# Queries and keys split once on 128 partitions and placed into the heads' stacked operands by transfers

## The chip, the cores and the metric

The kernel runs on one core of a Trainium2 chip. The metric is device time in microseconds (us) for one launch. Engines are named as in the profile: PE is TensorE (PEld its weight loads), DVE is VectorE, ACT is ScalarE, POOL is GpSimd, SP is SyncE, which here issues almost all transfers.

## The reference

One sequence of 512 tokens of width 1024 and 256 context tokens pass through two blocks of two layers each, all in float32. The first block's layers project to three kinds of heads, attend, project back and run an MLP with squared relu:

```python
q_a = _apply_rope(_heads(a_q, A_HEADS), cos64, sin64)
k_a = _apply_rope(_heads(a_k, A_KV_HEADS), cos64, sin64)
y_a = _window_attn(q_a, k_a, v_a, k_a_ctx, v_a_ctx, sink_a)
q_b = _apply_rope(_rms_norm(_heads(b_q, B_HEADS), q_norm_b), cos64, sin64)
k_b = _apply_rope(_rms_norm(_heads(b_k, B_KV_HEADS), k_norm_b), cos64, sin64)
...
def mla_q(cq):
    q = _heads(_rms_norm(cq, mla_q_norm) @ w_uq, C_HEADS)
    return q[..., :C_NOPE_DIM], q[..., C_NOPE_DIM:]
...
y = jnp.concatenate([_merge(y_a), _merge(y_b), _merge(y_c)], axis=-1) @ w_out
```

A heads (4 of 64, with 2 key heads) attend in a window with a sink, B heads (4, with 2 key heads) and C heads (8, with 64 rows without and 32 with rotation) to all 768 tokens. The second block's first layer adds a differential attention and a hyena (a gated long convolution), its second a pool over windows; both have MLPs:

```python
def _diff_attn(q, k, v, lam):
    s = jnp.einsum("bqhcd,bkhcd->bhcqk", q, k, preferred_element_type=jnp.float32) * (ATT_QK_DIM ** -0.5)
    p = jax.nn.softmax(s, axis=-1)
    w = p[:, :, 0] - lam * p[:, :, 1]
    return jnp.einsum("bhqk,bkhd->bqhd", w.astype(v.dtype), v)
```

## The kernel before

Activations stand with features on partitions and tokens in the row (512, or 768 with the context). Every operand of a product is kept as two float32r parts, hi and lo: `split` writes hi with ACT and lo = x − hi with DVE. `mm3` (L649) makes the products hi·hi, hi·lo and lo·hi of each 128-row piece; L656 is their matmul. Weights come through `Stream` in pieces of 128x1024: a load on SP (L79), hi on ACT (L97), lo on DVE (L98).

For queries and keys of 64 rows the two parts of a head are stacked on the 128 partitions, so that one product takes both. `k_post` (L753) writes for each of two key heads the rows [hi; lo] (L762, L763) and [lo; hi] (L764, L765), `q_post` (L740) for each of two query heads [hi; lo] (L749, L750). All of these are operations on 64 partitions, and those that cross halves read one half and write the other. `stack_key` (L1488, L1489) and `stack_query` (L1497 to L1500) do the same for the differential attention's keys and queries, `c_pair` (L877) prepares two C heads, rows [64; 32], from PSUM by `split` (L662, L663 for keys, L665, L666 for queries). The rotated 32 rows are made in u and w and go into the operands by transfers (`dma`, L669, on SP), as the keys' rotated rows kr do.

Tiles come from pools: `Tm` gives one of 4 slots of 128x768 (raw and temporary values: w, u, kx, qx, lam, the first component's probabilities), `B` one of 21 slots of 128x1536. A slot is taken again once the last reader of what it held is done.

Work is written unit by unit. `attend` (L916) runs units of 128 queries of one head as a pipeline: scores (L264), maximum (DVE L277), exponential (ACT L287), normalising (POOL L296), transposes (L310), their split (ACT L337, DVE L342), products with the values (L353). B heads come first, then A, then C; the pairs of C heads are prepared by `prepare` in steps between the units of the heads before:

```python
start = nab * 5 // 8 if p == 0 else nab + (p - 1) * per + 4
if i == start:
    gens[p] = prepare(p)
```

Beside the projections and the attention run background jobs: `mod_job` (weights wm loaded by SP, L597; multiplied on POOL, L580; summed on ACT, L581, or on DVE, L584), `context_job` (the differential attention's context keys) and the filter's job. In `mixer` (L1666) the keys, values and queries of the differential attention are projected between the steps of the hyena's chain (L1840: ka, x0, hy); then lam is loaded (L1772), and attention 2 begins. A scheduler sets each engine's order of instructions once, when the program is built; at run time each engine, SP included, works through its list in order.

Of the kernel before, what the change touches and what calls it, by code (L numbers as in the profile page):

```python
# [11 lines left out]
F32 = mybir.dt.float32  # L12
F32R = mybir.dt.float32r
# [51 lines left out]
class Stream:  # L65
    """Weight pieces [128, 1024] in the order of their use: loaded ahead, split into two float32r parts."""
# [45 lines left out]
class SideStream:  # L112
    """Weight pieces [128, 512] for work beside the main stream, three to a slot of the big pool."""
# [19 lines left out]
class Packer:  # L133
    """Views of a fixed width, several to a slot of the pool."""
# [17 lines left out]
class LayerNorm:  # L152
    """Norm over the rows of z (8 tiles of 128 rows) for one range of tokens; stats of the sums run with the producer."""
# [44 lines left out]
class RmsNorm:  # L198
    """Norm without mean; the squares are summed as the producer goes, the last ones (or all) by products."""
# [30 lines left out]
class Pair:  # L230
    """Transposed probabilities of two blocks of queries: [key, slot, 256 queries], hi and lo."""
# [9 lines left out]
class Unit:  # L241
    """One block of 128 queries of one head against its keys (or, for the context, both blocks at once)."""
# [74 lines left out]
    def parts(self):  # L317
        """(psum view, destination slots) of this block's transposed probabilities."""
# [45 lines left out]
class DiffUnit(Unit):  # L364
    """One block of 128 queries of one component of a differential head; the second one combines the two."""
# [39 lines left out]
class Kernel:  # L405
# [19 lines left out]
    def psum(self, pairs, singles):  # L425
        """PSUM as so many pairs of banks and so many single ones."""
# [6 lines left out]
    # ---------------------------------------------------------------- tiles  # L433
# [30 lines left out]
    def norm_space(self, n):  # L464
        """Three rows of n; two narrow ones that follow each other share a slot."""
# [8 lines left out]
    # ---------------------------------------------------------------- background  # L474
# [13 lines left out]
    def run(self, gen, rate=0, jobs=0):  # L488
        """gen, with so many steps of modulation and of other jobs (on average) after each of its own."""
# [9 lines left out]
    def weave(gens):  # L499
        """The generators' steps in turn."""  # L500
# [8 lines left out]
    @staticmethod  # L509
    def drain(gen):  # L510
        """Runs a generator to its end and returns its value."""
        while True:
            try:
                next(gen)
            except StopIteration as e:
                return e.value
# [7 lines left out]
    # ---------------------------------------------------------------- start  # L524
# [30 lines left out]
    def bcast(self, v, slot):  # L555
        """sbc[:, slot, :] = silu vector v on every partition."""
# [1672 lines left out]
```

## Time and profile before

| what | value |
|---|---|
| three runs | 3031.02, 3032.82, 3033.07 us; median 3032.82 |
| profiled execution | span 3033.6 us, 0.8 us above the median; its time outside the span is not listed apart |
| granted TensorE clock, mean | 0.964 of full speed |
| busy share of the span | PE 92%, DVE 68%, ACT 42%, POOL 26% |
| data moved | 327.80 MB, mean 108 GB/s |

The profiled execution is one run of its own. Busy shares are means over stages with different limits; what an edit is worth is read from its stage. In the rows below a line with `x4` is a group of four instructions of one kind that followed each other, with its first start and their total time, and the brackets at a line's end give the idle time before it and what ended that.

### The profile page before, as it was taken

To read this page: it belongs to the slowest core of one execution; us is meant where nothing else is said; L and a number is where in the kernel's file an instruction comes from. 1 tells how busy PE (TensorE), PEld (TensorE's weight loads), DVE (VectorE), ACT (ScalarE), POOL (GpSimd) and SP (SyncE) were. 2 spreads that over 40 slices of the span, in tenths; PEclk is the share of its full clock that TensorE was granted. 3 is DMA by queue.
4 is the path that set the end of the run, shared out by engine and by line. 5 is a ranking of instruction groups with operands and counts; after the bars stand their busy time and mean duration, and the time that the engine had idled before them with its cause. 6 is when DMAs were issued, how large, how long until landed. Compare 5 with 4: busy or idle time off the path is not lost.

```text
span 3033.6 us, 39799 instructions
## 1 busy us (share of the span) xinstructions
PE 2802.4 (92%) x14828; PEld 2352.8 (78%) x14828; DVE 2072.6 (68%) x3213; ACT 1262.5 (42%) x2282; POOL 777.9 (26%) x870
## 2 busy tenths in 40 slices
PE   6868989999999989888999999988899999699998
PEld 4757878888888878777887788766688888588887
DVE  5788876776556676887687565677976754764444
ACT  3557883412222235777332333533653223343222
POOL 4354456401000060343601122343211000400001
PEclk8979999999999999999999999999999999799999
DMA  5320122254444411012255565333125533123332
GB/s 233 106 77 12 35 82 70 91 154 145 150 131 129 125 63 60 11 33 73 64 174 178 177 204 174 102 128 108 59 68 193 200 124 98 46 84 97 96 97 71
DMA packets 102492, 327.80 MB, mean 108 GB/s; under 512 B 11643, under 2 KB 18747, under 8 KB 102300
## 3 DMA queue, kind: packets, MB, share of 16 engines
q1 hardware_dynamic: 101724, 323.56, 33.1%
q8 instruction: 117, 1.92, 0.3%
q10 hardware_dynamic: 576, 1.70, 0.2%
q14 instruction: 75, 0.61, 0.1%
HBM read 306.09 MB, written 13.37 MB: 105 GB/s over the span
## 4 chain that ended last, share of the span: by engine, by line
PE 70%; DVE 13%; issue 6%; ACT 5%; POOL 3%; DMA 2%; SPq 0%; DVEq 0%; POOLq 0%; ACTq 0%
PE f L656 47%; PE op L656 6%; PE pj L656 5%; PE s L264 3%; PE acc L353 2%; PE pt L310 1%; ACT p L287 1%; DVE st L277 1%; DVE h L1081 1%; DVE wlo L98 1%; DVE ptl L342 1%; DVE junk L584 1%; ACT pth L337 1%; PE lv L187 1%; DVE R L181 1%
## 5 line engine op out<-in xcount | busy, mean ns | idle before, releaser
L97 ACT CAST whi<-wraw 128x1024 fp32r<-128x1024 f32 x342 | 357.8, 1047 | 1190.7 <-PE f L656 1007.8
L656 PE MATMUL f<-hn,whi 128*128 128x512 f32 (+1 forms) x2688 | 716.9, 364 | 8.3 <-ACT hn L1082 6.3
L98 DVE TENSOR_TENSOR wlo<-wraw,whi 128x1024 fp32r<-128x1024 f32 x342 | 433.8, 1268 | 355.8 <-ACT whi L97 348.6
L656 PE MATMUL f<-act,whi 128*128 128x512 f32 x2240 | 613.0, 371 | 2.6 <-DVE R L983 2.6
L656 PEld LDWEIGHTS f<-hn,whi 128*128 128x128 f32 x2688 | 466.7, 190 | 95.1 <-ACT hn L1082 8.4
L656 PEld LDWEIGHTS f<-act,whi 128*128 128x128 f32 x2240 | 390.5, 189 | 79.7 <-DVE R L983 4.2
L656 PE MATMUL f<-hn,wlo 128*128 128x512 f32 (+1 forms) x1344 | 445.7, 361 | 0.0
L656 PE MATMUL f<-act,wlo 128*128 128x512 f32 x1120 | 377.7, 370 | 0.0
L570 POOL COPY wm<-act 128x1 f32<-128x1 f32 x152 | 81.1, 540 | 826.5 <-ACT act L945 419.3
L983 DVE SCALAR_TENSOR_TENSOR R<-f,modsb,R 128x512 f32<-128x512 f32 (+1 forms) x280 | 188.7, 693 | 130.8 <-PE f L656 130.6
L584 DVE SCALAR_TENSOR_TENSOR wm<-wm,sbc 128x1024 f32<-128x1024 f32 x152 | 186.5, 1228 | 128.2 <-DMA wm<-wada_in 80.7
L656 PEld LDWEIGHTS f<-hn,wlo 128*128 128x128 f32 x1344 | 237.2, 189 | 39.3
L656 PE MATMUL pj<-h,whi 128*128 128x512 f32 x864 | 241.1, 379 | 21.9 <-ACT h L662 17.7
L656 PEld LDWEIGHTS f<-act,wlo 128*128 128x128 f32 x1120 | 194.5, 188 | 36.7
L656 PEld LDWEIGHTS pj<-h,whi 128*128 128x128 f32 x864 | 151.1, 193 | 59.5 <-ACT h L662 19.0
L296 POOL TENSOR_SCALAR p<-p,st 128x768 f32<-128x768 f32 (+2 forms) x160 | 132.4, 831 | 195.1 <-DVE st L294 159.1
L277 DVE TENSOR_REDUCE st<-s 128x1 f32<-128x768 f32 (+3 forms) x176 | 155.9, 889 | 24.8 <-PE s L264 17.4
L342 DVE TENSOR_TENSOR ptl<-pt,pth 128x256 fp32r<-128x256 f32 (+3 forms) x304 | 152.8, 535 | 23.2 <-ACT pth L337 20.7
L218 POOL TENSOR_TENSOR ns<-ns,rq 128x256 f32<-128x256 f32 x54 | 46.9, 878 | 455.4 <-ACT rq L210 454.5
L310 PE MATMUL pt<-ident,p 128*128 128x128 f32 x816 | 127.0, 285 | 21.5 <-POOL p L296 13.1
L656 PE MATMUL pj<-h,wlo 128*128 128x512 f32 (+1 forms) x432 | 141.4, 370 | 0.0
L337 ACT CAST pth<-pt 128x256 fp32r<-128x256 f32 (+3 forms) x304 | 128.7, 471 | 30.1 <-PE pt L310 21.9
(375 smaller groups left out, 4836.1 us busy)
## 6 DMA issues: line engine op xcount, KB each, us to landing
wraw<-fc_in SPq DMA_DIRECT2D x128, 512.0 KB, 3.8
wraw<-mlp_in SPq DMA_DIRECT2D x128, 512.0 KB, 3.6
wm<-wada_in SPq DMA_DIRECT2D x96, 512.0 KB, 3.9
wm<-wmod_in SPq DMA_DIRECT2D x80, 512.0 KB, 3.8
wraw<-win_in SPq DMA_DIRECT2D x24, 512.0 KB, 3.7
wraw<-wout_in SPq DMA_DIRECT2D x16, 512.0 KB, 3.8
wraw<-mixhy_in SPq DMA_DIRECT2D x12, 512.0 KB, 3.7
wn<-wmodn_in SPq DMA_DIRECT2D x8, 512.0 KB, 7.7
```

The costliest lines, as they stand in the source:

```text
L97: nc.scalar.copy(out=hi[:, 0:n], in_=t[:, 0:n])
L98: nc.vector.tensor_tensor(out=lo[:, 0:n], in0=t[:, 0:n], in1=hi[:, 0:n].bitcast(F32), op=ALU.subtract)
L264: nc.tensor.matmul(self.s[:, a:b], lhsT=q, rhs=kk[:, k0:k0 + b - a], start=i == 0, stop=end)
L277: nc.vector.tensor_reduce(out=self.st[:, 0:self.nq], in_=s, axis=AX.X, op=ALU.max, negate=True)
L296: nc.gpsimd.tensor_scalar(out=self.p[:, b * m:b * m + m], in0=self.p[:, b * m:b * m + m], scalar1=st[:, 6 + b:7 + b], scalar2=1.0, op0=ALU ...
L310: nc.tensor.transpose(self.pt[t // w][:, t % w * 128:t % w * 128 + 128], self.p[:, t * 128:t * 128 + 128], k.ident)
L337: self.k.nc.scalar.copy(out=pr.hi[:, s0:s0 + c, q0:q0 + nq], in_=src)
L342: self.k.nc.vector.tensor_tensor(out=pr.lo[:, s0:s0 + c, q0:q0 + nq], in0=src, in1=pr.hi[:, s0:s0 + c, q0:q0 + nq].bitcast(F32), op=ALU.su ...
L570: self.nc.gpsimd.tensor_copy(out=t[:, 0:1], in_=self.gate)
L584: nc.vector.scalar_tensor_tensor(out=junk, in0=t, scalar=1.0, in1=s, op0=ALU.mult, op1=ALU.mult, accum_out=dst)
L656: self.nc.tensor.matmul(ps[:, c0:c1], lhsT=w, rhs=x[:, c0:c1], start=first and n == 0, stop=last and n == 2)
L983: nc.vector.scalar_tensor_tensor(out=zz, in0=ps[:, c0:c1], scalar=g(m0 + mi), in1=zz, op0=ALU.mult, op1=ALU.add)
```

## The change

A helper `halves` splits a tile of two heads once, on all 128 partitions: hi into a slot of `Tm`, lo in place of the tile. The parts are then copied into the stacked operands by transfers on SP, one for each 64 rows. The diff also takes out comments and docstrings; line numbers after it are up to 12 higher.

```diff
+    def halves(self, X, n, scale=None):
+        hi, lo = self.Tm("hs")[:, 0:n].bitcast(F32R), X[:, 0:n].bitcast(F32R)
+        self.split(hi, lo, X[:, 0:n], scale)
+        return hi, lo
...
     def q_post(self, X, q2, N, ranges, gain):
...
+        hi, lo = self.halves(X, N, SC64)
         for hd in range(2):
             a, b = slice(64 * hd, 64 * hd + 64), slice(64 - 64 * hd, 128 - 64 * hd)
-            x, hi = X[a, 0:N], q2[a, hd, 0:N]
-            nc.scalar.activation(out=hi, in_=x, func=AF.Copy, scale=SC64)
-            nc.vector.scalar_tensor_tensor(out=q2[b, hd, 0:N], in0=x, scalar=SC64, in1=hi.bitcast(F32), op0=ALU.mult, op1=ALU.subtract)
+            self.dma(q2[a, hd, 0:N], hi[a])
+            self.dma(q2[b, hd, 0:N], lo[a])
...
     def k_post(self, X, kk, gain):
...
+        hi, lo = self.halves(X, T)
         for hd in range(2):
             a, b = slice(64 * hd, 64 * hd + 64), slice(64 - 64 * hd, 128 - 64 * hd)
-            x, hi = X[a, :], kk[hd][a, 0, :]
-            nc.scalar.copy(out=hi, in_=x)
-            nc.vector.tensor_tensor(out=kk[hd][b, 0, :], in0=x, in1=hi.bitcast(F32), op=ALU.subtract)
-            nc.scalar.copy(out=kk[hd][b, 1, :], in_=x)
-            nc.vector.tensor_tensor(out=kk[hd][a, 1, :], in0=x, in1=hi.bitcast(F32), op=ALU.subtract)
+            self.dma(kk[hd][a, 0, :], hi[a])
+            self.dma(kk[hd][b, 0, :], lo[a])
+            self.dma(kk[hd][b, 1, :], hi[a])
+            self.dma(kk[hd][a, 1, :], lo[a])
...
     def c_pair(self, wq, wkv, cq, ckv, kr, j, qs, ks, ranges):
...
+        parts = [self.Tm("cq")[:, 0:N].bitcast(F32R) for _ in range(2)]
+        self.split(*parts, pn[:, 0:N], SC96)
         for i in range(2):
-            self.split(qs[i][0:64, 0, 0:N], qs[i][0:64, 1, 0:N], pn[64 * i:64 * i + 64, 0:N], SC96)
+            for n in range(2):
+                self.dma(qs[i][0:64, n, 0:N], parts[n][64 * i:64 * i + 64])
...
+        parts = [self.Tm("ck").bitcast(F32R) for _ in range(2)]
+        self.split(*parts, pk[:, 0:T])
         for i in range(2):
-            self.split(ks[i][0:64, 0, :], ks[i][0:64, 1, :], pk[64 * i:64 * i + 64, 0:T])
+            for n in range(2):
+                self.dma(ks[i][0:64, n, :], parts[n][64 * i:64 * i + 64])
             self.dma(ks[i][64:96, :, :], kr[64:96, :, :])
...
     def stack_key(self, x, d):
+        hi, lo = self.halves(x, x.shape[-1])
...
-            nc.scalar.copy(out=d[c][own], in_=x[own])
-            nc.vector.tensor_tensor(out=d[c][oth], in0=x[own], in1=d[c][own].bitcast(F32), op=ALU.subtract)
+            self.dma(d[c][own], hi[own])
+            self.dma(d[c][oth], lo[own])
...
     def stack_query(self, x, d, e):
+        hi, lo = self.halves(x, x.shape[-1], SC64)
...
-            hi = d[c][own].bitcast(F32)
-            nc.scalar.activation(out=d[c][own], in_=x[own], func=AF.Copy, scale=SC64)
-            nc.scalar.activation(out=e[c][oth], in_=x[own], func=AF.Copy, scale=SC64)
-            nc.vector.scalar_tensor_tensor(out=d[c][oth], in0=x[own], scalar=SC64, in1=hi, op0=ALU.mult, op1=ALU.subtract)
-            nc.vector.scalar_tensor_tensor(out=e[c][own], in0=x[own], scalar=SC64, in1=hi, op0=ALU.mult, op1=ALU.subtract)
+            self.dma(d[c][own], hi[own])
+            self.dma(d[c][oth], lo[own])
+            self.dma(e[c][oth], hi[own])
+            self.dma(e[c][own], lo[own])
```

How the change moves instructions is shown at three places. The first is the start of layer 0's attention. On DVE, before (kk are the stacked keys of the B heads, q_1072 and q_1073 the stacked queries of the A heads, raw the projected tiles, s scores):

```order
L763 TENSOR_TENSOR kk<-raw,kk 64x768
L765 TENSOR_TENSOR kk<-raw,kk 64x768
L763 TENSOR_TENSOR kk<-raw,kk 64x768
L765 TENSOR_TENSOR kk<-raw,kk 64x768
L738 TENSOR_TENSOR raw<-raw,w 128x512 x2
L277 TENSOR_REDUCE st<-s 128x1
L750 SCALAR_TENSOR_TENSOR q_1072<-raw,q_1072 64x768 x2
L750 SCALAR_TENSOR_TENSOR q_1073<-raw,q_1073 64x768 x2
```

and on DVE now:

```order
L663 TENSOR_TENSOR raw<-raw,hs 128x768
L737 TENSOR_TENSOR w<-rot,tab 128x512
L738 TENSOR_TENSOR raw<-raw,w 128x512
L737 TENSOR_TENSOR w<-rot,tab 128x512
L738 TENSOR_TENSOR raw<-raw,w 128x512
L666 SCALAR_TENSOR_TENSOR raw<-raw,hs 128x768
L584 SCALAR_TENSOR_TENSOR junk,modsb<-wm,sbc 128x1024
L666 SCALAR_TENSOR_TENSOR raw<-raw,hs 128x768
```

Four operations on kk have become one, four on q two. On SP the place now reads, at its end, where kk are the A heads' (before, eight wm loads stood there one behind the other, with no transfer of kk or q):

```order
L669 DMA kk<-hs 64x768
L669 DMA kk<-raw 64x768
L669 DMA kk<-hs 64x768
L669 DMA kk<-raw 64x768
L597 DMA wm<-wmod_in 128x1024 x3
L669 DMA qc<-cq 64x768 x4
L669 DMA kc<-kr 32x1536
```

Three of the wm loads now stand behind the 24 placing transfers of that place. The second place is SP in layer 1's attention, where a pair of C heads is prepared (qc, kc are the heads' operands, w and u the two parts of the rotated rows). Before:

```order
L669 DMA kc<-kr 32x1536 x2
L669 DMA qc<-w 32x512
L669 DMA qc<-u 32x512
L669 DMA qc<-w 32x512
L669 DMA qc<-u 32x512
L669 DMA kc<-kr 32x1536
```

and now:

```order
L669 DMA qc<-cq 64x512 x4
L669 DMA kc<-kr 32x1536
L669 DMA qc<-w 32x512
L669 DMA qc<-u 32x512
L669 DMA qc<-w 32x512
L669 DMA qc<-u 32x512
L669 DMA kc<-ck 64x768 x4
L669 DMA kc<-kr 32x1536
```

The keys' four pieces stand behind the four of the rotated rows. The third place is SP ahead of attention 2. Before:

```order
L79 DMA wraw<-mixq_in 128x1024 x2
L79 DMA wraw<-mixout_in 128x1024 x4
L1772 DMA lam<-lam_in 128x256
L1820 DMA hyr<-hy 128x512 x4
L1317 DMA R<-xb 128x512 x8
```

and the end of it now (hs and qx are hi and lo of a query tile, q_18707 and q_18708 stacked operands):

```order
L669 DMA q_18707<-hs 64x512
L669 DMA q_18707<-qx 64x512
L669 DMA q_18708<-hs 64x512
L669 DMA q_18708<-qx 64x512
L1783 DMA lam<-lam_in 128x256
L79 DMA wraw<-mixout_in 128x1024 x2
L1831 DMA hyr<-hy 128x512 x4
```

The load of lam has moved behind all 32 transfers of the queries.

## Rows read from the trace of the kernel before

**Rows 1.** page: busy time by engine, and the chain's shares by engine

```profile
PE 2802.4 (92%) x14828; PEld 2352.8 (78%) x14828; DVE 2072.6 (68%) x3213; ACT 1262.5 (42%) x2282; POOL 777.9 (26%) x870
PE 70%; DVE 13%; issue 6%; ACT 5%; POOL 3%; DMA 2%; SPq 0%; DVEq 0%; POOLq 0%; ACTq 0%
```

**Rows 2.** stretches: us, busy by engine (x count), granted clock, DMA share, GB/s

```profile
178.00:200.00 22.00, 9.95 (x20) 4.62 (x20) 19.34 (x20) 11.18 (x16) 12.79 (x7) 0.64 0.21 65
1224.00:1240.00 16.00, 9.21 (x36) 6.88 (x36) 14.47 (x24) 11.15 (x21) 4.50 (x5) 0.68 0.10 33
1280.00:1420.00 140.00, 123.90 (x778) 107.08 (x776) 110.67 (x236) 101.87 (x246) 56.50 (x64) 0.94 0.18 50
2127.00:2145.00 18.00, 10.73 (x46) 7.89 (x46) 17.28 (x33) 9.94 (x20) 4.02 (x4) 0.81 0.11 37
2700.00:2800.00 100.00, 100.00 (x443) 82.81 (x442) 48.07 (x56) 30.23 (x38) 0.00 (x0) 1.00 0.33 98
```

**Rows 3.** lines: durations ns min/median/max, first and last start, forms

```profile
L763 DVE TENSOR_TENSOR kk<-raw,kk x8: 952/954/3025, 186.2 to 1231.8; 64x768 fp32r<-64x768 f32 x8
L663 DVE TENSOR_TENSOR ckv<-raw,ckv x2: 954/956/959, 117.2 to 1174.0; 128x768 fp32r<-128x768 f32 x2
L666 DVE SCALAR_TENSOR_TENSOR qc<-cn,qc x16: 673/816/960, 273.3 to 1392.3; 64x768 fp32r<-64x768 f32 x8, 64x512 fp32r<-64x512 f32 x8
```

**Rows 4.** DMA issues: queue, count, KB each, median us to landing

```profile
kc<-kr SPq DMA_DIRECT2D x16, 192.0 KB, 2.7
qc<-w SPq DMA_DIRECT2D x8, 96.0 KB, 2.1
lam<-lam_in SPq DMA_DIRECT2D x1, 128.0 KB, 3.4
```

**Rows 5.** tile qc, SP's issues from 260 to 420: durations ns

```profile
L669 SPq DMA_DIRECT2D qc<-w x8: 507/519/582, 283.4 to 402.6; - x8
```

**Rows 6.** timeline of VectorE and POOL: start, us, engine, line, operation

```profile
186.22 3.02 DVE L763 TENSOR_TENSOR kk<-raw,kk 64x768 fp32r<-64x768 f32 x1
189.28 1.91 DVE L765 TENSOR_TENSOR kk<-raw,kk 64x768 fp32r<-64x768 f32 x1
195.37 3.91 DVE L750 SCALAR_TENSOR_TENSOR q<-raw,q 64x768 fp32r<-64x768 f32 x4
209.74 0.95 DVE L765 TENSOR_TENSOR kk<-raw,kk 64x768 fp32r<-64x768 f32 x1
186.09 2.34 POOL L580 TENSOR_TENSOR wm<-wm,sbc 128x1024 f32<-128x1024 f32 x1
1230.23 1.56 DVE L765 TENSOR_TENSOR kk<-raw,kk 64x768 fp32r<-64x768 f32 x1
```

**Rows 7.** timeline of TensorE and ScalarE, start of layer 0's attention

```profile
189.39 1.62 PE L264 MATMUL s<-kk,q 128*128 128x512 f32 x4 [1.61 <-DVE kk L763]
198.41 1.65 PE L264 MATMUL s<-kk,q 128*128 128x512 f32 x4 [5.46 <-ACT p L287]
193.90 3.44 ACT L749 ACTIVATE q<-raw 64x768 fp32r<-64x768 f32 x4 [4.29 <-DVE raw L738]
```

**Rows 8.** TensorE's waits from 1280 to 1420: us, times, longest

```profile
PE s L264 <- ACT p L287: 7.2, 6, 3.0
PE pt L310 <- POOL p L296: 5.1, 6, 1.0
```

**Rows 9.** timeline of SP, VectorE, TensorE: layer 1's third pair

```profile
1371.94 0.51 SPq L669 DMA_DIRECT2D qc<-w  x1
1372.77 0.96 DVE L663 TENSOR_TENSOR kc<-ck,kc 64x768 fp32r<-64x768 f32 x1
1374.01 2.32 PE L264 MATMUL s<-kc,qc 96*128 96x512 f32 x12
```

**Rows 10.** timeline of SP and VectorE at the start of attention 2

```profile
2128.64 0.42 SPq L1772 DMA_DIRECT2D lam<-lam_in  x1
2138.98 1.00 DVE L381 SCALAR_TENSOR_TENSOR p<-p,st,p 128x768 f32<-128x768 f32 x1
```

More of the change, by code (lines that the diff above doesn't have):

```diff
@@ L1483, in stack_key @@
     def stack_key(self, x, d):
-        nc = self.nc
+        hi, lo = self.halves(x, x.shape[-1])
         for c in range(2):
             own, oth = slice(64 * c, 64 * c + 64), slice(64 - 64 * c, 128 - 64 * c)
-            nc.scalar.copy(out=d[c][own], in_=x[own])
-            nc.vector.tensor_tensor(out=d[c][oth], in0=x[own], in1=d[c][own].bitcast(F32), op=ALU.subtract)
+            self.dma(d[c][own], hi[own])
+            self.dma(d[c][oth], lo[own])
     def stack_query(self, x, d, e):
-        nc = self.nc
+        hi, lo = self.halves(x, x.shape[-1], SC64)
         for c in range(2):
             own, oth = slice(64 * c, 64 * c + 64), slice(64 - 64 * c, 128 - 64 * c)
-            hi = d[c][own].bitcast(F32)
-            nc.scalar.activation(out=d[c][own], in_=x[own], func=AF.Copy, scale=SC64)
-            nc.scalar.activation(out=e[c][oth], in_=x[own], func=AF.Copy, scale=SC64)
-            nc.vector.scalar_tensor_tensor(out=d[c][oth], in0=x[own], scalar=SC64, in1=hi, op0=ALU.mult, op1=ALU.subtract)
-            nc.vector.scalar_tensor_tensor(out=e[c][own], in0=x[own], scalar=SC64, in1=hi, op0=ALU.mult, op1=ALU.subtract)
+            self.dma(d[c][own], hi[own])
+            self.dma(d[c][oth], lo[own])
+            self.dma(e[c][oth], hi[own])
+            self.dma(e[c][own], lo[own])
     def sine(self, ps, b, f, out):
```

## The prediction

> **What bounds the kernel now.** I read the page's busy times and its chain first. TensorE is busy 92% of the span and the chain of waits runs through it for 70%, through VectorE for 13%, ScalarE 5%, transfers 2% [rows 1]. So removed VectorE and ScalarE work pays only in stretches where TensorE stands still. I next read busy times by stretch [rows 2]. In the MLPs (2700 to 2800) TensorE is busy all 100 us: the four context keys that the change touches are prepared beside such work, and I cost them at nothing. Four places are otherwise: the start of attention 1 in layer 0 (178 to 200: TensorE 9.95 of 22 us, VectorE 19.34), the same in layer 1 (1224 to 1240: 9.21 against 14.47 of 16), the C heads' attention (1280 to 1420: 123.90 against 110.67 of 140) and the start of attention 2 (2127 to 2145: 10.73 against 17.28 of 18). The granted clock there is a mean between its two levels (1.2 and 2.4 GHz): 0.64 to 0.81 in the three starts, where TensorE had waited, and 0.94 in the attention.
>
> **What one edit saves.** Two 64-partition operations become one of 128 partitions with as long a row. The row length alone sets the time: the 64x768 subtraction takes 954 ns at the median, as a 128x768 one does (956) [rows 3]. So each pair that goes saves one full duration: 0.95 us (kk, kc), 0.82 (q, 768 long) or 0.68 (512 long) [rows 3]. Counted over the program, 56 operations go on VectorE and 56 on ScalarE: 8 from q_post, 12 from k_post, 16 from c_pair, 8 from stack_key, 12 from stack_query. At 0.68 to 0.95 us that is 38 to 53 us per engine, of spans with cover for most.
>
> **What one edit costs.** 192 transfers are added to SP. An issue takes 0.52 us at the median [rows 5], 100 us in all on a queue that has room, but pieces that follow each other start some 0.6 us apart, and none is usable before it lands: 2.7 us from issue for 192 KB, 2.1 for 96 KB [rows 4]. The new 64x768 pieces are 192 KB, so I take 2.7; the ends are 2.1 (half the bytes) and 3.4 (lam's 128 KB, from memory). The Trainium skill ("DMA: Bandwidth & Descriptors", section on the anatomy of one DMA) gives about 2.0 us plus the bytes at 436 GB/s, for GpSimd's path; for 192 KB that is an estimate of 2.45. By it every landing would come 0.25 us sooner, and the sum with its about ten exposed landings 2 to 3 us lower; the row, which is of SP's own transfers, decides.
>
> **Layer 0's start.** VectorE's first kk operations took 3.02 and 1.91 us there, two more 0.95 each, and q's four 3.91; four further kk operations end at 210.7 with one of 0.95 [rows 6]. Of this the change leaves one kk operation each time and two for q: 3.02 + 1.91 + 0.95 + 0.95 less about 2 (between 0.95 and 3.02), 3 x 0.95, and 1.95; some 9.5 us less VectorE work. Against it, TensorE's first scores come at 189.39, right behind the first kk operation [rows 7]. By the changed order a lo part is followed by four pieces of which the first scores need two hi and lo ones: 1.2 to 1.8 us of issues plus 2.7 us, so about 191.5 to 194 unless the single subtraction ends sooner. The third group of scores (198.41) waited 5.46 us for ACT's exponentials, which stood behind q's four hi parts (3.44 us there, now half) [rows 7]. The three modulation loads, moved behind 24 pieces, push POOL's and VectorE's share of that job away from this place. I take half of the 9.5 back and lose the landing partly: **−4 us**, between −9 (all the work was on the path) and +4 (nothing was, and both landings are).
>
> **Layer 1's start.** Four kk operations of 4.4 us (1.56 the longest [rows 6]) become one, q's two one: 3.4 + 0.7 us less in a stretch with VectorE busy nine tenths. The first landings are partly hidden, since TensorE there works on heads already prepared. **−3 us**, between −4 and +2.
>
> **The C heads.** Per layer 8 operations leave VectorE (4 x 0.95 + 4 x 0.68 or 0.82, 6.5 to 7.1 us) and 8 ScalarE. TensorE stands still for 16 of 140 us, 12.3 of it behind exponentials (7.2) and normalised probabilities (5.1) [rows 8], to which both engines contribute. A fifth to a half of the saving should arrive: −1.5 to −3.5 a layer. Against it stands the handover to each new pair, three times a layer. In layer 1's third pair the first piece of the rope part was issued at 1371.94, the last lo part ended at 1373.73, and the scores began at 1374.01 [rows 9], 2.07 us behind that piece: transfer and subtraction arrived together. In the changed order four ck pieces stand on SP behind the four rope pieces, so head a's two leave at about 1374.4 and 1375.0 and land 2.1 to 2.7 us later, 1376.5 to 1377.7. That is +2.5 to +3.7 at the old times, and +1 to +2 after the 1.6 us that one qc and one kc operation save ahead of them. Where the pair is prepared early, nothing. Six handovers at +0.8, less 2.3 a layer: **0 us**, between −7 (all hidden) and +14 (six at 3.4, less 6).
>
> **Mixer.** Hyena's ka and x0 loads and the bias vb now wait on SP behind key pieces (8 or 16 issues); VectorE loses 4 operations. **0**, between −3 and +4, from the 5 to 10 us of such issues and 4 x 0.68.
>
> **Attention 2's start.** The lam load was issued at 2128.64, and the difference of the probabilities began at 2138.98 [rows 10]. Now it stands behind all 32 query pieces; the last lo part was due near 2135, six to eight issues follow, so it leaves at about 2137 to 2138 and lands 3.4 us later [rows 4]: 2141 and two short operations, some 2.7 us late. The three or four subtractions saved there (0.68 each) give 2.1 back. **+1**, between −2 and +5. These pieces also hold their tiles of the four-slot pool until they have landed, and the first component's probabilities come from the same pool.
>
> **Sum:** −4 − 3 + 0 + 0 + 1 = −6 against the profiled execution's span of 3033.6 us (the table), which is 0.8 above the median of 3032.8; so 3027.6 there and **3027** as a median. A measurement of this kernel tells about 0.2%, 6 us, from no change.
>
> **Rivals.**
> 1. *Slower: the handovers of the C heads.* Six times TensorE runs dry while ck's pieces queue behind the rope's. For it: landing and subtraction met within 0.3 us in [rows 9], and the queue is in order. Against: the pipeline prepares some pairs well ahead. It decides once the lateness is above 2.5 us each: 6 x 3.4 = +20, less about 8 from the starts and the operations saved: **3045**. Chance 0.27.
> 2. *Larger gain: relief of VectorE and POOL.* kk's first operation took 3.02 us instead of 0.95 while POOL multiplied from 186.09 for 2.34 us; the last of its kind, at 209.74, took 0.95 [rows 6]. Fewer operations meet POOL, and ScalarE's exponentials come sooner throughout the C heads. Starts −9 − 4, attention −3.5 a layer, rest 0: **3013**. Chance 0.2. The Trainium skill ("SBUF — State Buffer", section on SBUF's two separate sides) says that a VectorE operation with two SBUF inputs and a GpSimd one that reads SBUF lock a shared port against each other for the whole instruction; this pair of durations agrees.
> 3. *No net change.* Landings take what the operations give, or TensorE's waits are set by the exponentials anyway: **3033**, within 4. Chance 0.13.
>
> That the change does not do what it says I leave out: the order has the 192 transfers and 56 fewer operations on each of the two engines.
>
> **How the numbers follow.** The forecast (0.4) spreads 6 us either way around 3027, so half of it lies more than 6 us below the median, half within 6. Faster: 0.2 + 0.2 = 0.40. Same: 0.2 + 0.12 of rival 3 = 0.32. Slower: 0.27 + 0.01 = 0.28. The range takes in rivals 2 and 1 to about their middle and leaves a tenth on each side: 3011 to 3046; the forecast's own is 3021 to 3033.
>
> **What would show it.** Right: VectorE busy 38 to 53 us lower with 56 fewer operations, a placed piece landing in 2.1 to 2.7 us, layer 0's first scores 2 to 4 us after 189.4 but that stage's end earlier, and TensorE's idle time in the C heads unchanged. Wrong: gaps of over 2.5 us ahead of each pair's first scores, with a transfer of ck as releaser (rival 1); or POOL and VectorE durations back at 0.95 and the starts 13 us shorter (rival 2). A stall on a tile of the four-slot pool that waits for a piece's landing would be a cause that I have not priced.

## The result and the profile after

The changed kernel takes **3048.82 us** (median of 4 runs, 3044.94 to 3050.2); the kernel before, beside it, 3032.86 (4 runs, 3031.02 to 3033.07). The ratio is 1.0056, 95% interval 1.0041 to 1.0072: 0.56% slower, clear of noise, where 3027 was forecast, and 3 us beyond the range's upper end of 3046. The profiled execution's span is 3048.4 us against 3033.6, 14.8 more.

The page of the changed kernel, parts 1 and 4 (the lines of [rows 1]):

```profile
PE 2806.2 (92%) x14828; PEld 2357.7 (77%) x14828; DVE 2024.8 (66%) x3157; ACT 1223.8 (40%) x2226; POOL 774.4 (25%) x870
PE 44%; DVE 7%; issue 4%; ACT 3%; POOL 2%; DMA 2%; SPq 1%; DVEq 0%; ACTq 0%; POOLq 0%
```

VectorE has 56 instructions and 47.8 us less, ScalarE 56 and 38.7 us less, as the change says. TensorE is busy 4 us longer with the same 14828 matmuls, and the span grows by 15: most of the saved work was not on the path. The chain's shares can't be compared with those before, since they add up to 63% of the span here and to 99% there: the chain was followed back over a part of the span only.

To see where, I cut the span at the same products of both kernels (TensorE's first matmul of a kind, from the timelines): the first projection, the first scores, the first product of the first pair of C heads (cn), the first product of the out-projection (op), and so on, to TensorE's last product.

| stage | before, us | after, us | difference |
|---|---|---|---|
| layer 0, projections to the first scores | 160.2 | 160.8 | +0.6 |
| layer 0, A and B heads (first scores to first cn) | 80.3 | 76.6 | −3.7 |
| layer 0, C stage (first cn to first op) | 180.4 | 186.9 | **+6.5** |
| layer 0, out-projection and MLP | 665.6 | 664.7 | −0.9 |
| layer 1, projections to the first scores | 106.4 | 110.8 | **+4.4** |
| layer 1, A and B heads | 60.6 | 58.2 | −2.4 |
| layer 1, C stage | 151.8 | 160.8 | **+9.0** |
| from there to the mixer's spectra (us) | 559.8 | 559.4 | −0.4 |
| mixer, to the first scores of attention 2 | 133.9 | 131.9 | −2.0 |
| attention 2, to the first product behind it | 91.3 | 94.6 | +3.3 |
| the rest, to TensorE's last product | 804.5 | 805.1 | +0.6 |

They make +15.0; with 0.6 us less ahead of the first stage that is 14.4 of the 14.8. The two C stages alone make 15.5. Their rows, before (layer 1, layer 0, then layer 1's projections and attention 2):

```profile
1282.70:1434.50 151.80, 133.73 (x845) 115.47 (x845) 120.31 (x250) 113.52 (x271) 61.51 (x71) 0.94 0.18 50
269.60:450.10 180.50, 156.95 (x1033) 136.87 (x1031) 140.22 (x289) 141.29 (x358) 86.88 (x111) 0.95 0.18 53
1115.70:1222.10 106.40, 101.47 (x516) 80.66 (x517) 73.93 (x102) 54.12 (x85) 24.84 (x27) 0.98 0.21 64
2128.20:2219.40 91.20, 77.95 (x520) 67.70 (x519) 85.87 (x157) 60.25 (x112) 24.18 (x25) 0.96 0.21 65
```

and after, in the same order (columns as in [rows 2]):

```profile
1286.60:1447.40 160.80, 137.19 (x845) 119.26 (x845) 115.65 (x242) 107.96 (x263) 62.72 (x70) 0.92 0.31 79
266.00:452.90 186.90, 159.51 (x1032) 139.31 (x1031) 134.67 (x280) 135.52 (x350) 88.04 (x111) 0.93 0.32 84
1117.60:1228.40 110.80, 103.59 (x517) 81.99 (x517) 68.16 (x96) 49.66 (x79) 24.96 (x27) 0.97 0.32 89
2138.70:2233.40 94.70, 80.08 (x521) 69.50 (x519) 84.12 (x154) 58.55 (x109) 24.49 (x25) 0.93 0.29 85
```

In layer 1's C stage VectorE loses 4.7 us of work and ScalarE 5.6, and TensorE's idle time (the stage less its busy time) rises from 18.1 to 23.6 us. Its busy time rises too, by 3.5 us for the same 845 matmuls: the mean granted clock falls from 0.94 to 0.92, so a part of the stage more runs at 1.2 instead of 2.4 GHz. In layer 0's C stage idle time rises from 23.6 to 27.4 us, and busy time by 2.6. So of the loss in the two stages 9.4 us are idle time and 6.0 busy time.

The handover to layer 1's third pair, after (timelines of SP, VectorE, ScalarE and TensorE; [rows 9] before):

```profile
1378.69 0.54 SPq L669 DMA_DIRECT2D qc<-w  x1
1381.28 2.46 SPq L669 DMA_DIRECT2D kc<-ck  x4
1378.57 0.78 ACT L662 CAST ck<-ck 128x768 fp32r<-128x768 f32 x1
1379.38 0.96 DVE L663 TENSOR_TENSOR ck<-ck 128x768 fp32r<-128x768 f32 x1
1382.03 0.37 ACT L356 COPY yt<-acc 64x256 f32<-64x256 f32 x1 [2.69 <-DMA qc<-w]
1382.85 0.44 PE L310 MATMUL pt<-ident,p 128*128 128x128 f32 x2 [3.21 <-ACT y L358]
1383.94 4.12 PE L264 MATMUL s<-kc,qc 96*128 96x512 f32 x12 [0.65 <-issue]
```

Two things arrive late at once. The keys' first piece, a hi part, leaves at 1381.28, behind the four rope pieces, 1.93 us after ScalarE had made it (1379.35), and the scores follow 2.66 us after it; that piece took 2.6 us to land, so the scores began when it had. And ScalarE's copy of an earlier head's result (yt, which takes its place from the same four-slot pool as cq, ck, u and w) waits 2.69 us until a rope transfer has read its slot; the transposes behind it wait 3.21 us for that copy's partner y, and stand ahead of the scores in TensorE's list. Before, the scores stood 2.07 us behind the rope part's first transfer; now 5.25. The landing ended last: without yt's wait the scores would have begun no sooner.

TensorE's largest wait in the whole stage (us in total, times, longest), before:

```profile
PE s L264 <- ACT p L287: 7.0, 5, 3.0
```

and its largest waits after:

```profile
PE acc L353 <- DVE st L294: 7.0, 2, 3.6
PE s L264 <- ACT p L287: 5.4, 5, 1.6
PE pt L310 <- ACT y L358: 3.2, 1, 3.2
```

The wait for exponentials has shrunk from 7.0 us to 5.4. The 7.0 us at acc are not all new, nor a wait for a transfer. They are two stops, at the handovers to the second and fourth pair. At the fourth, before and after:

```profile
1397.21 2.29 DVE L98 TENSOR_TENSOR wlo<-wraw,whi 128x1024 fp32r<-128x1024 f32 x1
1402.58 0.78 PE L264 MATMUL s<-kc,qc 96*128 96x512 f32 x2 [3.03 <-ACT p L287]
```

```profile
1408.80 2.29 DVE L98 TENSOR_TENSOR wlo<-wraw,whi 128x1024 fp32r<-128x1024 f32 x1
1414.69 1.18 PE L353 MATMUL acc<-pth,vc 128*128 128x256 f32 x6 [3.45 <-DVE st L294]
```

In both kernels VectorE runs the split of a weight piece (L98, 2.29 us), u's part, a maximum and a key part without a pause, and only then ptl, the lo part of the transposed probabilities, for which the value products (acc) wait; the row names st, the short operation that ended last ahead of them. The exponentials before wait for that maximum. Before, the new pair's scores came next in TensorE's list and were done in turns with the value products. After, the scores stand behind the value products and the transposes, and TensorE stops a second time, 1.61 us, between two groups of scores. By the idle time between the pairs' first cn products (5.5, 3.9, 3.0 and 5.7 us before, 5.6, 6.1, 4.8 and 7.2 after) the handovers to the second, third and fourth pair cost 2.2, 1.8 and 1.5 us more.

The page's DMA issues, after ([rows 4] before):

```profile
kc<-ck SPq DMA_DIRECT2D x32, 192.0 KB, 3.3
kk<-hs SPq DMA_DIRECT2D x16, 192.0 KB, 3.7
kk<-raw SPq DMA_DIRECT2D x16, 192.0 KB, 4.0
kc<-kr SPq DMA_DIRECT2D x16, 192.0 KB, 3.5
q<-hs SPq DMA_DIRECT2D x24, 128.0 KB, 2.3
```

The pieces of 192 KB land in 3.3 to 4.0 us at the median, where I took 2.7. The unchanged kr transfers, now among them, went from 2.7 to 3.5. It is the later ones of a series that take longer: in the third pair above, the first ck piece landed in 2.6 us, the second in 3.2, the fourth in 3.8, and kr behind them in 3.8.

### The profile page after: what moved, and what is told of

Same layout as the page of the kernel before. It is cut to its first block, busy times and chain, and to the rows that moved or that the text cites. A ratio compares the mean times of both kernels' runs of the same rounds, so it can differ in the third digit from the quotient of the medians.

```text
span 3048.4 us, 40142 instructions
## 1 busy us (share of the span) xinstructions
PE 2806.2 (92%) x14828; PEld 2357.7 (77%) x14828; DVE 2024.8 (66%) x3157; ACT 1223.8 (40%) x2226; POOL 774.4 (25%) x870
## 4 chain that ended last, share of the span: by engine, by line
PE 44%; DVE 7%; issue 4%; ACT 3%; POOL 2%; DMA 2%; SPq 1%; DVEq 0%; ACTq 0%; POOLq 0%
PE f L656 30%; PE op L656 3%; PE pj L656 3%; PE s L264 2%; PE acc L353 1%; PE pt L310 1%; DVE st L277 1%; DMA wm<-wada_in 1%; DVE gt L1874 1%; DVE ptl L342 1%; PE fs L1577 1%; SPq L669 1%; PE ck L1449 0%; ACT p L287 0%; POOL ns L218 0%
## 5 line engine op out<-in xcount | busy, mean ns | idle before, releaser
L98 DVE TENSOR_TENSOR wlo<-wraw,whi 128x1024 fp32r<-128x1024 f32 x342 | 433.8, 1269 | 360.8 <-ACT whi L97 353.8
L584 DVE SCALAR_TENSOR_TENSOR wm<-wm,sbc 128x1024 f32<-128x1024 f32 x152 | 186.1, 1225 | 127.1 <-DMA wm<-wada_in 80.3
L656 PEld LDWEIGHTS pj<-h,whi 128*128 128x128 f32 x864 | 151.8, 193 | 61.1 <-ACT h L662 19.0
L287 ACT ACTIVATE p<-s,st 128x768 f32<-128x768 f32 (+2 forms) x160 | 126.0, 789 | 52.3 <-DVE st L277 40.6
```

The lines of the kernel that those rows point to most:

```text
L98: nc.vector.tensor_tensor(out=lo[:, 0:n], in0=t[:, 0:n], in1=hi[:, 0:n].bitcast(F32), op=ALU.subtract)
L287: nc.scalar.activation(out=self.p[:, b * m:b * m + m], in_=self.s[:, self.c0 + b * m:self.c0 + b * m + m], func=AF.Exp, bias=st[:, b:b + 1 ...
L584: nc.vector.scalar_tensor_tensor(out=junk, in0=t, scalar=1.0, in1=s, op0=ALU.mult, op1=ALU.mult, accum_out=dst)
L656: self.nc.tensor.matmul(ps[:, c0:c1], lhsT=w, rhs=x[:, c0:c1], start=first and n == 0, stop=last and n == 2)
```

## The experiments

**Theory A**: the loss arises in c_pair's handovers. **Rival B**: SP's queue as a whole. **Rival C**: layer 1's projections, carried on. Each result below has the whole program's ratio, and the C stages of layers 0 and 1 from its own trace. They are steadier than the whole, though not exact: four traces with c_pair as before in layer 0 gave 179.3 to 182.4 us, three in layer 1 151.3 to 153.1. Layer 0's out-projection and MLP, which no edit touches, took 656.9 to 665.6 us in the traces of the runs with two modulation buffers, before and after among the longest; single times of the kernel before ran from 3021.95 to 3038.53 us.

### c_pair as before, and c_pair alone

The first run restores c_pair in the changed kernel, the second puts the new one into the kernel before.

```diff
-        parts = [self.Tm("cq")[:, 0:N].bitcast(F32R) for _ in range(2)]
-        self.split(*parts, pn[:, 0:N], SC96)
         for i in range(2):
-            for n in range(2):
-                self.dma(qs[i][0:64, n, 0:N], parts[n][64 * i:64 * i + 64])
+            self.split(qs[i][0:64, 0, 0:N], qs[i][0:64, 1, 0:N], pn[64 * i:64 * i + 64, 0:N], SC96)
...
-        parts = [self.Tm("ck").bitcast(F32R) for _ in range(2)]
-        self.split(*parts, pk[:, 0:T])
         for i in range(2):
-            for n in range(2):
-                self.dma(ks[i][0:64, n, :], parts[n][64 * i:64 * i + 64])
+            self.split(ks[i][0:64, 0, :], ks[i][0:64, 1, :], pk[64 * i:64 * i + 64, 0:T])
```

> The change with c_pair as it was before (64-partition splits, 128 transfers fewer on SP than the change); q_post, k_post, stack_key and stack_query stay changed. Theory A (the loss arises in c_pair's handovers, where the two traces differ by +7.8 us in layer 0's attention behind its start and by +8.6 us in layer 1's): about 3048.4 less 16.4, 3032 us span, within 4 of the kernel before; no drift at the second, third and fourth pair. Rival B (SP's queue as a whole, so that transfers of all five functions cost alike): loss in proportion to the 64 transfers left of 192, about 3038. Rival C (the loss starts at the projections of layer 1, +6 us there, and is only carried on): 3044 or more.

Measured: 3027.15 us, ratio 0.9991 (0.9976 to 1.0006); C stages 179.5 and 153.1 us:

```profile
266.20:445.70 179.50, 156.90 (x1033) 136.87 (x1031) 140.83 (x289) 141.37 (x358) 86.57 (x111) 0.96 0.19 53
1273.40:1426.50 153.10, 134.95 (x844) 116.98 (x844) 119.78 (x250) 113.46 (x270) 61.42 (x70) 0.93 0.18 49
```

> The kernel before with c_pair alone changed. Theory A: about 3033.6 + 16 = 3050 us span, since the other parts gave and took a few us that cancel. Rival B: 3033.6 + 15 x 128/192 = 3044. Rival C: 3036 or less.

Measured: 3048.05 us, ratio 1.0056 (1.0036 to 1.0076); C stages 187.4 and 158.6 us. c_pair is enough for the whole loss, and without it the loss is gone. Rivals B and C fall. B's two expected times were worked out with 128 of the 192 transfers in c_pair; the trace has 64 (kc<-ck x32, qc<-cq x32), so the two change places, about 3044 for the first run and 3039 for the second, and it falls with these too. The other four functions together give and take about nothing.

### Its key part and its query part

> The change with c_pair's query part undone, its key part still split on 128 partitions and placed by transfers. Theory A in the form that the key pieces, which stand behind the rope pieces on SP, and the slots that they and the rope tiles hold are the cause: loss nearly whole, 3043 to 3048 us. Rival (the query pieces hold two of the four slots that u and w wait for): 3034 to 3038.

Measured (query part as before, keys by transfers): 3042.14 us, ratio 1.0031 (1.0014 to 1.0048); C stages 183.6 and 159.2 us:

```profile
266.70:450.20 183.50, 157.67 (x1031) 139.69 (x1030) 136.39 (x284) 138.14 (x353) 87.34 (x111) 0.93 0.25 69
1276.90:1436.10 159.20, 135.81 (x844) 117.22 (x844) 116.89 (x247) 110.44 (x266) 63.09 (x70) 0.92 0.25 67
```

> The change with c_pair's key part undone, its query part still placed by transfers. Theory A with the key pieces as the cause: 3031 to 3037 us, no wait of a copy out of acc (yt) for a rope transfer. Rival (query pieces): 3043 to 3048.

Measured (key part as before, queries by transfers): 3028.99 us, ratio 0.9999 (0.9985 to 1.0013); its C stages:

```profile
265.20:450.50 185.30, 161.83 (x1033) 140.30 (x1031) 138.37 (x285) 139.02 (x354) 85.68 (x111) 0.93 0.25 69
1278.40:1428.00 149.60, 131.33 (x845) 114.50 (x845) 118.88 (x246) 111.09 (x267) 61.14 (x70) 0.95 0.25 64
```

In layer 1 the key part makes the loss (+6.1 on the first run's 153.1), and the query part alone is a gain (−3.5). In layer 0 both lose (+4.1 and +5.8), and together not more than 7.4. The query part's loss there is hardly idle time, which is 23.5 us against 22.6: it is busy time at a clock of 0.93 instead of 0.96.

TensorE's idle time says it more plainly than the stages' length. Here it is for each run in us, with the busy time and the mean granted clock in brackets:

| c_pair | layer 0's C stage | layer 1's C stage |
|---|---|---|
| as before: kernel before | 23.6 (157.0, 0.95) | 18.1 (133.7, 0.94) |
| as before: first run | 22.6 (156.9, 0.96) | 18.2 (135.0, 0.93) |
| as before: k_post as before too | 23.6 (155.7, 0.97) | 18.8 (132.5, 0.95) |
| keys by transfers | 25.8 (157.7, 0.93) | 23.4 (135.8, 0.92) |
| queries by transfers | 23.5 (161.8, 0.93) | 18.3 (131.3, 0.95) |
| both: c_pair alone | 27.3 (160.1, 0.93) | 23.7 (134.9, 0.92) |
| both: the change | 27.4 (159.5, 0.93) | 23.6 (137.2, 0.92) |

Idle time is the same within 1 us where c_pair is the same, and it adds up: against the first run the keys' part costs 3.2 and 5.2 us, the queries' part 0.9 and 0.1, both 4.8 and 5.4. Busy time differs by up to 2.5 us between traces with the same c_pair, as the granted clock does. With the parts that were kept (at the end of this section), layer 0's C stage had c_pair as before and a busy time of 159.6 us at 0.94. So the query part's 161.8 is little outside that spread, and the loss that is shown is the keys' idle time.

### The queue, the slots, the order

Two runs start from the fourth (operands written directly), and load SP's queue by transfers to memory that nobody reads, and then the pool as well, by sending them from two of its tiles. The second of the two, against the fourth run:

```diff
         for i in range(2):
             self.split(ks[i][0:64, 0, :], ks[i][0:64, 1, :], pk[64 * i:64 * i + 64, 0:T])
+        parts = [self.Tm("ck").bitcast(F32R) for _ in range(2)]
+        self.split(*parts, pk[:, 0:T])
+        for i in range(2):
+            for n in range(2):
+                self.dma(self.a["scr"].pop(), parts[n][64 * i:64 * i + 64])
```

> As the fourth run (c_pair's key part split on 64 partitions into the operands, as before), but each operand's part is also sent from there to memory by a transfer that nobody reads: four more transfers of 192 KB per pair on SP at the place of the change's key pieces, with no slot of the four-slot pool held and no product waiting for them. C stage (first product of the first pair's queries to the first out-projection) was 180.4 and 151.8 us before, 186.9 and 160.8 with the change, 185.2 and 149.6 in the fourth run. If products wait for landings, or if the slots are short: as the fourth run, 185 and 150 us, within 1.5. If SP's queue itself is what is short (whatever stands behind the pieces is late): 187 and 158 or more.

Measured (transfers read from kc, no tile held): 3036.74 us, ratio 1.0019 (1.0001 to 1.0037); C stages 188.1 and 151.4 us:

```profile
1279.10:1430.50 151.40, 130.25 (x844) 111.71 (x844) 117.52 (x246) 110.86 (x267) 60.25 (x70) 0.98 0.32 84
```

In layer 1 the queue costs 1.8 us, little; in layer 0 it costs 2.9 us, and there my division of the two cases came out on the queue's side. But in layer 0 TensorE's idle time is that of the fourth run (23.7 against 23.5 us), and its busy time, 2.6 us longer at 0.91 instead of 0.93, has moved no more than between traces with the same c_pair (3.9 us). In layer 1 idle time rises by 2.9 us, with a wait of 4.28 us for a kr piece that stood behind the idle transfers, and a higher clock (0.98) hides a part of it.

> As the run before it, but the idle transfers leave from two tiles of the four-slot pool, written by one 128-partition operation on ScalarE and one on VectorE more than the operands need. If only the landing in front of the scores costs: 185 to 187 and 150 to 152 us for the C stages. If the slots cost (a copy out of acc, yt, waits for a slot that a transfer still reads): 186 to 189 and 155 to 160, with that wait of 2 to 3 us in the trace at the handovers.

Measured: 3040.53 us, ratio 1.0034 (1.002 to 1.0048); C stages 188.0 and 156.5 us:

```profile
1287.30:1443.80 156.50, 136.25 (x845) 117.33 (x845) 121.99 (x250) 113.91 (x271) 61.15 (x70) 0.92 0.31 82
```

Layer 1 takes another 5.1 us with two slots held until transfers have read them, though no product waits for any of it (0.95 us of VectorE and 0.8 of ScalarE for each of four pairs is in this too). That does not show a cost of slots there: TensorE's idle time is 20.3 us, 0.9 less than in the run before, and the whole difference is busy time at a clock of 0.92 instead of 0.98. The expected wait of yt for a transfer does not show. In layer 0 the stage is as long as in the run before, but idle time rises from 23.7 to 28.0 us; whether by the slots or by the two more operations was not separated.

The third changes only SP's order of the change: the first head's pieces first.

```diff
+            if i == 0:
+                for n, part in enumerate((hi, lo)):
+                    self.dma(qs[1][64:96, n, 0:N], part[32:64, 0:N])
             self.dma(ks[i][64:96, :, :], kr[64:96, :, :])
```

> The change with SP's list in another order for each pair: rope pieces of the first head, key pieces of the first head, then those of the second head. The first head's key pieces leave 1.2 us sooner. If landings in front of the first scores set the handover: C stages 1.2 us shorter at two to three handovers each, 183 to 185 and 157 to 159 us. If slots or SP's queue as a whole: 186 to 187.5 and 160 to 161.5 us.

Measured: 3045.37 us, ratio 1.0038 (1.0023 to 1.0053); C stages 187.3 and 154.5 us:

```profile
1288.20:1442.70 154.50, 134.36 (x844) 116.83 (x844) 114.20 (x242) 107.20 (x262) 60.90 (x70) 0.93 0.33 83
```

Layer 1 gains 6.3 us, more than the 2 to 4 expected, 3.5 of it idle time; layer 0 gains nothing. So the place of the keys' pieces in the queue is a cause in layer 1. ScalarE's yt waits there for a rope transfer twice, 7.9 us in all, longer than in the change (2.7): that wait does not set the stage's length.

Then the pool itself: five slots, and a tile of its own for yt.

```diff
-        self.wm = P("wm", bufs=2)
+        self.wm = P("wm", bufs=1)
-        self.t = P("t", bufs=4)
+        self.t = P("t", bufs=5)
...
-        tmp = k.Tm("yt")[:, 0:256]
+        tmp = k.ya.tile([128, 256], F32, name="yt", tag="ya")
```

> The change with five slots instead of four in the pool of 128x768 tiles and a tile of its own for yt; the room comes from one modulation buffer instead of two, so only layer 1's C stage is read, where no modulation runs. It was 160.8 us with the change, 151.8 before. If held slots cost about 5 us, as the run with idle slots against the one with idle transfers says: 155 to 157. If only the landing ahead of the scores does: 160 to 161.

Measured: 3150.3 us as a whole, most of it in the stages with modulation, which lost a buffer (ratio 1.0385, 1.0362 to 1.0409); layer 1's C stage 151.3 us:

```profile
1365.10:1516.40 151.30, 130.48 (x845) 114.48 (x844) 113.74 (x242) 107.78 (x262) 61.25 (x70) 0.95 0.33 84
```

and its largest waits of TensorE:

```profile
PE s L264 <- ACT p L287: 8.1, 7, 1.7
PE acc L353 <- DVE ptl L342: 4.2, 5, 1.2
PE pt L310 <- POOL p L296: 2.4, 2, 1.3
```

> Both together: five slots with yt apart, and the first head's pieces first on SP. Layer 1's C stage: 150 to 153 us if slots and the key pieces' place are the two causes; near 154.5 (the reordered run) if slots add nothing.

Measured: 3142.88 us, ratio 1.0361 (1.0333 to 1.0389); layer 1's C stage 149.0 us:

```profile
1368.00:1517.00 149.00, 129.14 (x846) 113.28 (x845) 113.89 (x243) 107.88 (x263) 61.18 (x71) 0.97 0.33 86
```

With more room in the pool layer 1's stage is back at its old length, twice what I expected of it, with as many transfers as in the change. The waits at acc of 3.6 us and at pt of 3.2 us are gone, and none is longer than 1.7 but the last, of 1.9, at the out-projection, as in every run. With the better order the stage is 2.8 us shorter than before the change. But by idle time five slots take back 2.8 us (23.6 to 20.8), the better order 3.5 (to 20.1), both 3.7 (to 19.9), and 18.1 was the value before. The other 6.7 us of the five slots' gain are busy time at a clock of 0.95 instead of 0.92. And with five slots the scheduler also writes other lists: a key piece left ahead of the rope's at the third pair, and at the second pair VectorE's ptl came ahead of the keys' part. So **the order in which the key pieces and the scores come, and the room in the pool**, each lengthen the stage, and they overlap. That a wait for a held slot is what costs is not shown: the one such wait in the change's stage, yt's, ended before the scores' first key piece had landed. For layer 0 the test says nothing, since with one buffer modulation work reaches into that stage.

### Layer 1's projections

> The first run (c_pair as before) with k_post also as before. Layer 1's projections (first product to first scores) took 106.4 us before, 110.7 in the first run; its A and B heads (first scores to the first pair) 60.6 and 58.2. If the keys' eight pieces hold the first scores up: 107 to 108 for the projections, and 59 to 61 for the heads. If the queries' pieces do: 110 to 111 and 58 to 59. Layer 0's first scores at 189 us either way.

Measured: 3035.07 us, ratio 1.0019 (1.0006 to 1.0031); layer 1's projections 111.9 us, its A and B heads 59.3; layer 0's A and B heads 80.7 us instead of 76.0 in the first run. So q_post, not k_post, holds up layer 1's first scores, and k_post is what gains in layer 0's heads: 4.7 us.

### The parts that gained

q_post by transfers in layer 0 alone, k_post by transfers, c_pair's queries by transfers in layer 1 alone, its keys as before, stack_key and stack_query by transfers, lam loaded and worked out ahead of the queries:

```diff
+        if self.layer == 1:
+            parts = [self.Tm("cq")[:, 0:N].bitcast(F32R) for _ in range(2)]
+            self.split(*parts, pn[:, 0:N], SC96)
...
+        lm = self.Tm("lam")
+        nc.sync.dma_start(out=lm[:, 0:256], in_=a["lam"])
...
         qpk = Packer(self, 512, name="q2")
```

> Only the parts whose stages were shorter in the runs so far: k_post placed by transfers, q_post by transfers in layer 0 alone, c_pair's key part as before, its query part by transfers in layer 1 alone, stack_key and stack_query by transfers, and lam loaded and worked out ahead of the queries. By the stages of those runs against the kernel before: layer 0's A and B heads -4, its C stage -1, layer 1's projections 0 if the queries' pieces made the 4.4 us there (otherwise +4), its A and B heads -2.4, its C stage -2.2, mixer -3, attention 2 between 0 and +1 instead of +3.3: 12 us less, 3021 us span, ratio 0.996. If the gains hang on each other: 3026 to 3030.

Measured: **3017.88 us**, ratio **0.9946** (0.9932 to 0.996), faster than both kernels. Its profiled span is 16.8 us shorter than that of the kernel before (3016.8 against 3033.6); 6.8 of that lie in layer 0's out-projection and MLP, which vary so by themselves, and about 10 in the stages that the edits touch, where 12 were expected. Its C stages, layer 1's projections and attention 2:

```profile
266.40:448.80 182.40, 159.58 (x1033) 139.52 (x1031) 141.03 (x289) 141.56 (x358) 86.53 (x111) 0.94 0.18 52
1273.30:1423.00 149.70, 131.37 (x845) 114.58 (x845) 118.81 (x246) 111.28 (x267) 61.17 (x71) 0.95 0.24 64
1107.60:1214.00 106.40, 101.50 (x516) 80.70 (x517) 70.11 (x99) 51.66 (x82) 24.93 (x27) 0.98 0.27 78
2114.90:2203.80 88.90, 78.03 (x520) 67.46 (x519) 82.51 (x149) 58.16 (x108) 24.82 (x25) 0.98 0.31 90
```

Layer 1's projections are back at 106.4 with q_post as before there: it made all 4.4 us. Attention 2 takes 88.9 us where the change took 94.6, with lam's place the only difference of the code there. Layer 0's C stage, with c_pair as before in it, is the one that did not come as expected: 182.4 us against 179.5 in the first run. Its idle time is the same (22.8 and 22.6 us), its busy time is 2.7 us longer at a clock of 0.94 instead of 0.96; why the clock differs stays open.

## Why the prediction was wrong

- **Failing step: the C heads, put at 0 (−7 to +14), measured +15.5.** The sum was six handovers at +0.8, less 2.3 us a layer of saved work. All three of its parts failed. The *handovers*: by TensorE's idle time in the stretches from one pair's first cn product to the next, those to the second, third and fourth pair cost 2.4, 2.0 and 2.5 us in layer 0 and 2.2, 1.8 and 1.5 in layer 1, together 12.4 us, some 2.1 each. The *saving*: idle time fell by 3.0 us in layer 0's first stretch and by nothing in layer 1's, 2.9 in all instead of 4.6. The *clock*: the same products took 6.0 us more busy time at a lower granted clock (0.95 to 0.93, 0.94 to 0.92), which the sum had at nothing without a reason. A part of it is the spread between traces. 12.4 − 2.9 + 6.0 makes the measured 15.5. The prediction's own sign for being right, TensorE's idle time in the C heads unchanged, failed: 41.6 us became 51.0.
- **Why the handover was put too low.** The late key pieces themselves were foreseen: in the third pair the scores were to come 2.5 to 3.7 us later behind the rope's first transfer at the old times, and came 3.2 later (5.25 against 2.07), with a first piece that landed in 2.6 us, as priced. But 1.6 us were taken off for the operations saved ahead of it, and they did not arrive: from the pair's first cn product to its scores it was 15.6 us instead of 12.4. And the sum had only the landing; at the second and fourth pair TensorE's list itself had changed, and the scores came behind the value products. The pool's slots, which the prediction named as a cause not priced, show as a wait only at yt; five slots shortened the stage, but through other lists as well. How much each has of this stays open.
- **Rival 1** comes near in time (3045), but not by its sign: no wait ahead of a pair's first scores in the change has a transfer of ck as its releaser, though at the third pair a landing ended last.
- **A reading**: the 0.82 us for a query operation of 768 columns was the median over both lengths [rows 3]; those of 768 take 0.94 to 0.96. That moves the saving by less than 1 us.
- **Layer 1's start, put at −3 (−4 to +2), measured +2.0** (+4.4 − 2.4): wrong in sign, at the end of its range. I counted saved operations and landings; q_post cost 4.4 by neither. TensorE waits in layer 1's projections for a square that ScalarE makes for a head norm (sq), and the sum over it (pv):

```profile
PE pv L705 <- ACT sq L712: 4.1, 2, 3.5
```

This wait stands in every run with q_post by transfers in layer 1 and in none of the three without (before, c_pair alone, the kept parts). The square ran at 1194.69 before, ahead of the query parts; now it stands in ScalarE's list behind the second query tile's hi part, at 1201.84. Idle time rises by 2.3 us, busy time by 2.1 at a clock of 0.97 instead of 0.98. Both sq and hs come from the four-slot pool, but five slots did not remove the wait; why the list has this order was not traced.
- **Layer 0's start, put at −4, measured −3.1**: right in size. Its detail was wrong: the first scores came at 189.40 in both kernels, since the one subtraction was done 2.6 us sooner than the old first kk operation. Rival 2's relief did not show there either, that subtraction still took 2.00 us:

```profile
184.69 2.00 DVE L663 TENSOR_TENSOR raw<-raw,hs 128x768 fp32r<-128x768 f32 x1
```

- **Attention 2, put at +1 (−2 to +5), measured +3.3**: the mechanism was right, the size off. lam was issued at 2147.52, 2137.0 on the old times (the stage's first scores had shifted by 10.6), just where I had it. POOL waited 8.81 us, until it landed, and the difference of the probabilities began 14.3 us behind the first scores instead of 10.8, 3.5 late where I had 2.7. What failed is the 2.1 us that the saved subtractions were to give back: they did not show.

```profile
2147.52 0.59 SPq L1783 DMA_DIRECT2D lam<-lam_in  x1
2149.54 0.90 POOL L378 TENSOR_SCALAR p<-p,st 128x768 f32<-128x768 f32 x1 [8.81 <-DMA lam<-lam_in]
```

- **Mixer, put at 0, measured −2.0**, inside its range; the MLPs' 0 held within 1 us.
- **The range** ended at 3046 because the highest price was six handovers of 3.4 us less 8 us of gains. The gains came (layer 0's and 1's A and B heads together −6.1), but they were eaten by layer 1's projections and attention 2, which the slower rival had left at their likeliest values. Bounds of several terms on the slow side belong together when one queue and one pool feed them all.

The Trainium skill ("DMA: Bandwidth & Descriptors", section on the anatomy of one DMA) puts the fixed part of one DMA at about 2.0 us on GpSimd's path; with its rate the estimate for 192 KB was 2.45 us. The first piece of a series agrees roughly (2.6 us in the third pair), the medians of 3.3 to 4.0 us do not, so for transfers that follow each other on SP the measurement is the one to use.

## What to carry to other kernels

A copy that replaces a compute operation can cost more than its issue and landing. It holds its source until it has been read, and the scheduler writes other lists around it: here the new pair's scores fell behind the value products, and a square fell behind a query part. So look where the next product stands in TensorE's list, and count the slots of the pool and who else draws from them, before counting engine time. Cut both traces at the same products and compare stage by stage; the ratio alone showed one loss where there were four losses and three gains, each of 2 us or more, and keeping only the gains, with lam moved ahead, made 0.9946 of a change that was 1.0056. Then split each stage into TensorE's idle and busy time: idle time came out the same from trace to trace, busy time did not. A load that many later operations need (lam) is worth placing by hand ahead of a burst of transfers on the same queue: 5.7 us here (94.6 to 88.9).

## What was not expected of the hardware

Transfers of 192 KB issued 0.6 us apart land later than the first of them: 2.6, 3.2 and 3.8 us in one series; kr's, unchanged in size and number, went from 2.7 to 3.5 us, kk's take 3.7 to 4.0. And TensorE's busy time for the same products is not fixed: in layer 0's C stage, with c_pair as before, it was 155.7 to 159.6 us in four traces, at granted clocks of 0.97 to 0.94, with idle times of 22.6 to 23.6 us. With the query part by transfers it was 161.8 us at 0.93 and 23.5 us idle. So a longer stage with equal idle time can be the clock alone; what lowered it was not shown.
